# Probabilities times values in plain fp32, two key blocks in the two column halves of the array, inside a two-layer decoder trunk

## The chip, the cores and the metric

The kernel runs on one core of a Trainium2 chip. A time is the device time of one execution in microseconds (us). The kernel before takes 950.52 us, the median of three runs (949.91, 950.52 and 955.53). One more execution was profiled; it took 955.44 us, and every row of the trace below comes from that one. Its span, from the first to the last instruction, is 953.7 us.

## The reference, cut to what matters

The input is 256 tokens of width 1024 in float32. Two layers follow one another, each as half SwiGLU, mixer, half SwiGLU with RMSNorm around every part. The mixer of layer 0 is a pooling mixer. The mixer of layer 1 is an attention with three branches, and the change is in it:

```
proj = h @ w_in                       # q, and k and v of three branches, and gates
o_cmp = softmax(q . k_cmp) @ v_cmp    # 15 compressed keys
o_sel = softmax(q_rot . k_s) @ v_s    # selected blocks
o_win = softmax(q_rot . k_w) @ v_w    # window of 256
o = g0 * o_cmp + g1 * o_sel + g2 * o_win
return o @ w_o
```

There are 16 heads of 64 channels in 4 key groups of 4 heads. With 256 tokens there are 4 blocks of 64, and all are picked, so the selected branch and the window branch are both causal attention over the whole sequence, with their own keys and values. The product of the last softmax with the values, `P @ V`, is what changes in form.

## The kernel before, in words

All weights are float32 in device memory. A product of two float32 matrices is made of three matmuls in the chip's reduced float32 type (fp32r): an operand is split into a high part (a copy on ScalarE that rounds, line 309, or 294 for weights) and a low part (a subtraction on VectorE, line 310 or 295), and `mm3` (lines 304 to 306) adds high by high, high by low and low by high. Some small products are left in plain fp32 instead (lines 740, 758, 769, 802), and so are all transposes, which go through TensorE with an identity matrix (`csm`).

The trunk runs one stage after the other: two SwiGLU parts with the pooling mixer between them, then the SwiGLU part `ffn(1, 0)`, the attention `nsa`, and `ffn(1, 1)`. The attention runs from about 600 to 760 us of the span. Its steps stand in a list written by hand, `NSA_STEPS`; each entry emits one piece of work, and a planner that simulates the engines then orders the instructions of each engine, mostly in the order in which they were emitted, with pieces that are ready earlier let past. The engines work through their own queues in that order.

The names that matter: `t` is one of two halves of 128 queries, `g` one of four key groups (4 heads). `qk(t, g)` computes scores (line 849, each head pair in one half of the array's rows), adds the causal mask (851), takes the maximum on VectorE (853), exponentiates on ScalarE (855) and multiplies by the gate and the reciprocal sum on GpSimd (864). `pv(t, g)` makes `P @ V` for four heads at once into one PSUM tile `o` of 128 x 512. It begins with the compressed branch: GpSimd spreads the compressed probabilities `Pch` and `Pcl` over the heads with a mask (line 882, two instructions of 128 x 512), and two matmuls multiply them by `VC` (line 874). Then it goes through the key blocks of 128 keys, two branches times `t+1` blocks, so 2 blocks for t=0 and 4 for t=1, in all 24 over the eight (t, g). For each block there are four transposes into a PSUM tile (893), a split into `PTh` (309) and `PTl` (310), and two fp32r matmuls of 128 x 512 (874): one for the high, one for the low part of the probabilities. The 128 columns of the stationary operand hold the 64 channels of the high part of V and the 64 of its low part, so the two halves of `o` are added at the end: a copy of the upper half (909), two additions (911) and a split into `OT` (309, 310), which the output projection `out_proj` (304 to 306, `acc<-whi`) reads. Each `yield` ends one step of `NSA_STEPS`.

`v_post` splits V (lines 719), `cmp_v` splits VC (771), `q_pct` splits the compressed probabilities (821). PSUM has two pools of four tiles each; `o` and the transposes come from `psG`, the scores and the accumulators of the output projection from `psA`.

Of the kernel before, what the change touches and what calls it, by code (L numbers as in the profile page):

```python
# [9 lines left out]
F32 = mybir.dt.float32  # L10
F32R = mybir.dt.float32r
BF16 = mybir.dt.bfloat16
AF = mybir.ActivationFunctionType
OP = mybir.AluOpType
# [3 lines left out]
P = 128  # L18
S = 256
NT = S // P  # L20
# [5 lines left out]
NH, HD, NG, NR = 16, 64, 4, 4  # L26
# [72 lines left out]
    ("pv", 0, 1),  # L99
    ("pv", 0, 1),  # L100
    ("vcmp", 1, 0),
    ("pv", 1, 0),
    ("pct", 1, 0),
    ("qk", 1, 0),
    ("qk", 1, 0),
# [1 line left out]
    ("pv", 1, 0),  # L107
    ("pv", 1, 0),
    ("pv", 1, 0),
    ("qk", 1, 1),  # L110
    ("qk", 1, 1),
    ("pv", 1, 0),
    ("rope", 1, 1),
    ("pv", 1, 1),
    ("qk", 1, 1),
    ("qk", 1, 1),
    ("pv", 1, 1),
    ("pc", 1, 1),
    ("qk", 0, 2),
# [2 lines left out]
    ("pv", 1, 1),  # L122
    ("qk", 0, 2),
    ("pv", 1, 1),
    ("pv", 0, 2),
    ("pv", 1, 1),
    ("qk", 0, 3),
    ("qk", 0, 2),
    ("qk", 0, 3),
    ("pv", 0, 2),  # L130
    ("qk", 0, 3),
# [16 lines left out]
    ("out", 0, 0),  # L148
    ("qk", 1, 3),
    ("out", 1, 0),  # L150
    ("pv", 1, 3),
    ("qk", 1, 3),
    ("out", 0, 1),
    ("wo", 2, 0),
    ("out", 0, 2),
# [81 lines left out]
def _trunk(ctx: ExitStack, tc: tile.TileContext, d, out):  # L237
    nc = tc.nc
# [18 lines left out]
    bmask = csm[:, 322:330]  # L257
# [50 lines left out]
    def split(dst, src):  # L308
        return (nc.scalar.activation(dst[0], src, AF.Copy),  # L309
                nc.vector.tensor_tensor(dst[1], src, dst[0].bitcast(F32), op=OP.subtract))  # L310
# [333 lines left out]
    def nsa(pre, g_post, nxt, W0, preload):  # L644
        with tc.tile_pool(name="np", bufs=1, reuse_waits="tile") as np_:
# [11 lines left out]
            W2, W0 = W0  # L657
            gates = [np_.tile([P, 48], F32, name=f"gates{t}") for t in range(NT)]
            kT = tuple(np_.tile([P, NG, 2, S], F32R, name=f"kT{q}") for q in "hl")
            V = np_.tile([P, NT, 2, NG, 2, HD], F32R, name="V")  # L660
            pos = np_.tile([P, 2, 2, 8], F32, name="pos")
            nc.sync.dma_start(pos[:, 0], d["posk"].rearrange("p (a b) -> p a b", a=2))
            nc.sync.dma_start(pos[:, 1], d["posv"].rearrange("p (a b) -> p a b", a=2))
# [50 lines left out]
                            pos[ps, kv, ab, None, None, :].to_broadcast([64, NG, 8 - skip, 8]), op=OP.add)  # L714

            def v_post(o, t):
                ov = o.rearrange("p (b g e) -> p b g e", b=2, g=NG)
                for br in range(2):
                    split([V[:, t, br, :, q, :] for q in range(2)], ov[:, br])

            hidT = np_.tile([P, 2, 2, NG, 16], F32, name="hidT")
            kbd = np_.tile([P, NG, 2, 16], F32, name="kbd")
            VC = [np_.tile([P, 2, HD], F32R, name=f"VC{c}") for c in range(2)]

            def cmp_w(kv):
                src = d[("wk1", "wv1")[kv]]
# [36 lines left out]
            def cmp_v(c):  # L763
                pv = psG.tile([P, HD], F32, name="g")
                rep = np_.tile([P, 2, 2, NR, 16], F32, name="rep", bufs=1)
                for k in range(2):
                    nc.vector.tensor_copy(rep[:, k], hidT[:, 1, k, 2 * c:2 * c + 2, None, :].to_broadcast([P, 2, NR, 16]))
                for k in range(2):
                    nc.tensor.matmul(pv, rep[:, k].rearrange("p a b c -> p (a b c)"), wv2[:, k, :],
                                     start=k == 0, stop=k == 1)  # L770
                split([VC[c][:, q] for q in range(2)], pv)

            qT = {}
            PcT = {}
# [42 lines left out]
            def q_pct(c, t, e):  # L817
                pt = psG.tile([P, P], F32, name="g")
                nc.tensor.transpose(pt, e.rearrange("p a b -> p (a b)"), ident)
                pc = tuple(np_.tile([P, P], F32R, name=f"Pc{q}", bufs=3) for q in "hl")  # L820
                split(pc, pt)
                PcT[c, t] = pc

            OT = [None, None]
# [42 lines left out]
            def pv(t, g):  # L867
                c = g // 2
                Ps = PP[t, g]
                o = psG.tile([P, 2, 2, P], F32, name="g")  # L870

                def mm(A, hl, start, stop):
                    for j in range(2):
                        nc.tensor.matmul(o, A.rearrange("p a b -> p (a b)"), hl[j], start=start and j == 0, stop=stop and j == 1)  # L874

                def PT():
                    return tuple(np_.tile([P, 2, 2, P], F32R, name=f"PT{q}", bufs=2) for q in "hl")

                hl = PT()
                msk = bmask[:, 4 * (g % 2):4 * (g % 2) + 4].rearrange("p (b a) -> p a b", a=2)  # L880
                for q, w in zip(hl, PcT[c, t]):
                    nc.gpsimd.tensor_tensor(q, w[:, None, None, :].bitcast(F32).to_broadcast([P, 2, 2, P]),
                                            msk[:, :, :, None].to_broadcast([P, 2, 2, P]), op=OP.mult)
                mm(VC[c], hl, True, False)
                yield
                nblk = 2 * (t + 1)
                n = 0
                for br in range(2):
                    for kt in range(t + 1):
                        pt = psG.tile([P, 2, 2, P], F32, name="g")  # L890
                        for pr in range(2):
                            for par in range(2):
                                nc.tensor.transpose(pt[:, par, pr, :], Ps[pr][:, par * 2 + br, kt * P:(kt + 1) * P], ident)  # L893
                        hl = PT()
                        split(hl, pt)
                        n += 1
                        mm(V[:, kt, br, g], hl, False, n == nblk)
                        if n < nblk:
                            yield
                if OT[t] is None:  # L900
                    if t == 0:
                        ot = pp.tile([P, 2, 2, KD, P], F32R, name="xT")[:, 0]
                    else:
                        ot = np_.tile([P, 2, KD, P], F32R, name="ot1")
                    OT[t] = [ot[:, i] for i in range(2)]
                ol = np_.tile([P, 512], F32, name="y", bufs=3)
                of = np_.tile([P, 2, P], F32, name="of", bufs=1)
                ol = ol[:HD].rearrange("p (a b q) -> p a b q", a=2, b=2)
                nc.scalar.activation(ol, o[HD:], AF.Copy)
                for par in range(2):  # L910
                    nc.vector.tensor_tensor(of[par * HD:(par + 1) * HD], o[:HD, par], ol[:, par], op=OP.add)
                split([v[:, 2 * g:2 * g + 2, :] for v in OT[t]], of)
                yield
# [33 lines left out]
            def step(kind, i, j):  # L947
# [12 lines left out]
                elif kind == "gates":  # L960
                    gate_fix()
                elif kind == "vpost":
                    v_post(O[4, j], j)
                elif kind == "wcmp":
                    wc[i] = cmp_w(i)
                elif kind == "cmp":
                    hm[i] = cmp_mm(i, wc[i])
                elif kind == "hid":
                    cmp_hid(i, hm[i])
                elif kind == "kcmp":  # L970
                    cmp_k()
                elif kind == "vcmp":
                    cmp_v(i)
                elif kind == "q":
                    qs[i, j] = q_evac(O[3 + 2 * i, j])
                elif kind == "nope":
                    qn[i, j] = q_nope(qs[i, j])
                elif kind == "rope":
                    q_rope(i, j, qs[i, j])
                elif kind == "pc":  # L980
                    ec[i, j] = q_cmp(i, j, qn[i, j])
                elif kind == "pct":
                    q_pct(i, j, ec[i, j])
                elif kind == "wo":
                    wo.append(ksplit(piece(d["wo"][:, i * 2048:(i + 1) * 2048], step=512), 2))
                    if i == 3:
                        nxt.load()
                elif kind == "out":
                    out_proj(i, j)
# [18 lines left out]
    for c, hs, ls in ((0, [], pre[0].s), (1, [], pre[0].s), (2, pre[0].h[0], pre[0].h[0]), (3, pre[0].h[0], pre[0].h[0])):  # L1008
        v = [q[:, c * 512:(c + 1) * 512] for q in W[0]]
# [11 lines left out]
    W = ffn(0, 1, pre[2], 5, pre[3], W, pre_ffn(1, 0))  # L1021
    W = ffn(1, 0, pre[3], 7, pre[4], W, pre_nsa())
    W = nsa(pre[4], 9, pre[5], W, pre_ffn(1, 1))
    ffn(1, 1, pre[5], 11, None, W, None)

# [14 lines left out]
```

## Time and profile before

| what | value |
|---|---|
| runs | 949.91, 950.52, 955.53 us, median 950.52 us |
| profiled execution | 955.44 us, its span 953.7 us |
| TensorE matmul busy | 937.3 us, 98% of the span |
| VectorE busy | 666.1 us, 70% |
| ScalarE busy | 475.7 us, 50% |
| GpSimd busy | 82.2 us, 9% |
| mean granted TensorE clock | 0.988 |

In the profile PE stands for TensorE's matmuls, PEld for its weight loads, DVE for VectorE, ACT for ScalarE, POOL for GpSimd and SP for SyncE. Matmuls are pipelined, so the length of a record is longer than the distance to the next one; the distance between starts is what a matmul costs in a row of them. A granted clock (PEclk) of 1.00 is 2.4 GHz, one of 0.50 is 1.2 GHz. "128*64" in a matmul is the rows and columns of the array that it uses, and "128x512" the moving operand.

### The profile page before, as it was taken

To read this page: it belongs to the slowest core of one execution; us is meant where nothing else is said; L and a number is where in the kernel's file an instruction comes from. 1 tells how busy PE (TensorE), PEld (TensorE's weight loads), DVE (VectorE), ACT (ScalarE), POOL (GpSimd) and SP (SyncE) were. 2 spreads that over 40 slices of the span, in tenths; PEclk is the share of its full clock that TensorE was granted. 3 is DMA by queue.
4 is the path that set the end of the run, shared out by engine and by line. 5 is a ranking of instruction groups with operands and counts; after the bars stand their busy time and mean duration, and the time that the engine had idled before them with its cause. 6 is when DMAs were issued, how large, how long until landed. Compare 5 with 4: busy or idle time off the path is not lost.

```text
span 953.7 us, 13074 instructions
## 1 busy us (share of the span) xinstructions
PE 937.3 (98%) x4882; PEld 783.3 (82%) x4882; DVE 666.1 (70%) x977; ACT 475.7 (50%) x812; POOL 82.2 (9%) x78
## 2 busy tenths in 40 slices
PE   8999999999999999999999999999999999999997
PEld 5888888877888888888888888888677678888885
DVE  6866677786867666758666667688965868666653
ACT  7654444355645344545544444545765666544421
POOL 1000001131000000110000002002445110000000
PEclk9999999999999999999999999999889899999999
DMA  8865675325866565258665553572200358665511
GB/s 318 283 223 195 216 239 178 124 98 176 271 216 221 185 207 184 90 173 279 211 214 182 186 194 98 204 265 90 88 1 1 112 193 284 213 211 186 193 45 44
DMA packets 47457, 168.96 MB, mean 177 GB/s; under 512 B 5529, under 2 KB 6041, under 8 KB 46882
## 3 DMA queue, kind: packets, MB, share of 16 engines
q1 hardware_dynamic: 47394, 168.13, 52.7%
q8 instruction: 38, 0.62, 0.3%
q14 instruction: 25, 0.20, 0.1%
HBM read 167.06 MB, written 1.05 MB: 176 GB/s over the span
## 4 chain that ended last, share of the span: by engine, by line
PE 52%; DVE 4%; issue 1%; ACT 1%; DMA 0%; POOL 0%; DVEq 0%; POOLq 0%; ACTq 0%
PE g L501 14%; PE g L502 7%; PE acc L304 5%; PE acc L306 5%; PE acc L305 5%; PE g L304 3%; PE g L306 2%; PE g L305 2%; PE acc L849 2%; PE g L874 2%; PE g L469 1%; PE g L893 1%; DVE wlo L295 1%; PE acc L851 1%; DVE x L350 1%
## 5 line engine op out<-in xcount | busy, mean ns | idle before, releaser
L501 PE MATMUL g<-xT,whi 128*128 128x512 f32 x1152 | 406.0, 394 | 0.0
L502 PE MATMUL g<-xT,wlo 128*128 128x256 f32 x1152 | 325.1, 282 | 0.0
L294 ACT ACTIVATE whi<-raw 128x1024 fp32r<-128x1024 f32 (+2 forms) x252 | 204.9, 863 | 157.7 <-issue 41.8
L295 DVE TENSOR_TENSOR wlo<-raw,whi 128x1024 fp32r<-128x1024 f32 (+2 forms) x252 | 244.5, 1012 | 46.6 <-ACT whi L294 46.3
L501 PEld LDWEIGHTS g<-xT,whi 128*128 128x128 f32 x1152 | 216.3, 188 | 49.5
L502 PEld LDWEIGHTS g<-xT,wlo 128*128 128x128 f32 x1152 | 216.5, 188 | 1.4
L295 DVE TENSOR_TENSOR dlo<-raw,dhi 128x1024 fp32r<-128x1024 f32 (+1 forms) x128 | 119.3, 955 | 100.0 <-ACT dhi L294 99.9
L294 ACT ACTIVATE dhi<-raw 128x1024 fp32r<-128x1024 f32 (+1 forms) x128 | 103.9, 842 | 153.9 <-DMA raw<-in_wd 145.2
L438 DVE TENSOR_REDUCE sg<-g 128x256 f32<-128x512 f32 x144 | 98.1, 687 | 58.1 <-PE g L502 58.0
L304 PE MATMUL acc<-dhi,hTh 128*128 128x512 f32 x288 | 112.3, 390 | 0.0
L305 PE MATMUL acc<-dlo,hTh 128*128 128x512 f32 x288 | 112.0, 389 | 0.0
L306 PE MATMUL acc<-dhi,hTl 128*128 128x512 f32 x288 | 111.4, 389 | 0.0
L304 PE MATMUL g<-whi,xT 128*128 128x512 f32 (+2 forms) x168 | 64.4, 385 | 1.3 <-ACT xT L309 0.7
L341 POOL TENSOR_TENSOR rs<-ms,neghalf 128x1 f32<-128x1 f32 x24 | 13.2, 548 | 602.2 <-DVE ms L339 602.2
L305 PE MATMUL g<-wlo,xT 128*128 128x512 f32 (+2 forms) x168 | 63.9, 381 | 0.0
L306 PE MATMUL g<-whi,xT 128*128 128x512 f32 (+2 forms) x168 | 63.6, 380 | 0.0
L306 PEld LDWEIGHTS acc<-dhi,hTl 128*128 128x128 f32 x288 | 54.1, 188 | 11.4
L304 PEld LDWEIGHTS acc<-dhi,hTh 128*128 128x128 f32 x288 | 54.1, 188 | 11.2
L305 PEld LDWEIGHTS acc<-dlo,hTh 128*128 128x128 f32 x288 | 54.0, 188 | 9.9
L304 PEld LDWEIGHTS g<-whi,xT 128*128 128x128 f32 x168 | 31.9, 190 | 8.4 <-ACT xT L309 2.0
L305 PEld LDWEIGHTS g<-wlo,xT 128*128 128x128 f32 x168 | 32.0, 191 | 6.5 <-DVE wlo L295 0.8
L306 PEld LDWEIGHTS g<-whi,xT 128*128 128x128 f32 x168 | 32.0, 190 | 6.5 <-DVE xT L310 0.7
(191 smaller groups left out, 1044.0 us busy)
## 6 DMA issues: line engine op xcount, KB each, us to landing
raw<-in_wu SPq DMA_DIRECT2D x88, 512.0 KB, 4.6
raw<-in_wd SPq DMA_DIRECT2D x88, 512.0 KB, 4.5
raw<-in_wg SPq DMA_DIRECT2D x86, 512.0 KB, 3.9
raw<-in_win SPq DMA_DIRECT2D x18, 512.0 KB, 4.5
gain<-in_gains SPq DMA_DIRECT2D x11, 512.0 KB, 3.7
raw<-in_wo SPq DMA_DIRECT2D x8, 512.0 KB, 5.0
raw<-in_win SPq DMA_DIRECT2D x4, 304.0 KB, 2.9
raw<-in_wg SPq DMA_DIRECT2D x4, 256.0 KB, 3.7
```

The costliest lines, as they stand in the source:

```text
L294: nc.scalar.activation(hi[:, n + a:n + b], r[:, a:b], AF.Copy)
L295: nc.vector.tensor_tensor(lo[:, n + a:n + b], r[:, a:b], hi[:, n + a:n + b].bitcast(F32), op=OP.subtract)
L304: nc.tensor.matmul(o, A[0], B[0], start=start, stop=False)
L305: nc.tensor.matmul(o, A[0], B[1], start=False, stop=False)
L306: return nc.tensor.matmul(o, A[1], B[0], start=False, stop=stop)
L341: nc.gpsimd.tensor_tensor(r, v, neghalf, op=OP.pow)
L350: nc.vector.scalar_tensor_tensor(x[t][:, H[h]], fg[:, H[h]], r, x[t][:, H[h]], op0=OP.mult, op1=OP.add)
L438: nc.vector.tensor_reduce(dst, o.rearrange("p a b -> p b a"), axis=AX.X, op=OP.add)
L501: nc.tensor.matmul(o, hi, pre.xx[:, :, k, :], start=k == 0, stop=False)
L502: nc.tensor.matmul(o[:, 1, :], lo, xT[0][:, k, :], start=False, stop=k == KD - 1)
L849: nc.tensor.matmul(o, A[i], B[j], start=i + j == 0, stop=False)
L874: nc.tensor.matmul(o, A.rearrange("p a b -> p (a b)"), hl[j], start=start and j == 0, stop=stop and j == 1)
```

## The change

The low and high parts of probabilities and values go away. `V`, `VC`, the compressed probabilities and the transposed probabilities `PT` are plain fp32 copies. `pv` takes the key blocks in pairs: eight transposes into two PSUM tiles, one copied out by ScalarE and the other by VectorE, a `yield`, then two fp32 matmuls of 128 x 512 with 64 stationary columns each, one into partitions 0 to 63 of `o` and the other into partitions 64 to 127, which are the two column halves of the array, and a `yield`. The compressed branch moves from the first step of `pv` to its last: one GpSimd instruction in place of two, and two fp32 matmuls of 128 x 256, one in each column half. The end of `pv`, which adds the two halves of `o`, stays. The number of steps of a `pv` stays too (3 for t=0, 5 for t=1), but in `NSA_STEPS` some `pv` steps move back by one to four entries, past `qk`, `rope` and `pct` steps; no step that issues a DMA is moved.

```diff
 NSA_STEPS = [
...
-    ("pv", 1, 0),
     ("pct", 1, 0),
     ("qk", 1, 0),
     ("qk", 1, 0),
...
     ("pv", 1, 0),
     ("pv", 1, 0),
+    ("pv", 1, 0),
     ("qk", 1, 1),
...
-            V = np_.tile([P, NT, 2, NG, 2, HD], F32R, name="V")
+            V = np_.tile([P, NT, 2, NG, HD], F32, name="V")
...
             def v_post(o, t):
-                ov = o.rearrange("p (b g e) -> p b g e", b=2, g=NG)
-                for br in range(2):
-                    split([V[:, t, br, :, q, :] for q in range(2)], ov[:, br])
+                nc.scalar.activation(V[:, t].rearrange("p b g e -> p (b g e)"), o, AF.Copy)
...
-                split([VC[c][:, q] for q in range(2)], pv)
+                nc.vector.tensor_copy(VC[c], pv)
...
-                split(pc, pt)
+                nc.scalar.activation(pc, pt, AF.Copy)
...
             def pv(t, g):
                 c = g // 2
                 Ps = PP[t, g]
                 o = psG.tile([P, 2, 2, P], F32, name="g")
...
+                of32 = o.rearrange("p a b q -> p (a b q)")
+                blocks = [(br, kt) for br in range(2) for kt in range(t + 1)]
+                for n in range(0, len(blocks), 2):
+                    PT = []
+                    for i, (br, kt) in enumerate(blocks[n:n + 2]):
                         pt = psG.tile([P, 2, 2, P], F32, name="g")
                         for pr in range(2):
                             for par in range(2):
                                 nc.tensor.transpose(pt[:, par, pr, :], Ps[pr][:, par * 2 + br, kt * P:(kt + 1) * P], ident)
-                        hl = PT()
-                        split(hl, pt)
-                        n += 1
-                        mm(V[:, kt, br, g], hl, False, n == nblk)
-                        if n < nblk:
-                            yield
+                        q = np_.tile([P, 512], F32, name="PT", bufs=6)
+                        v = pt.rearrange("p a b q -> p (a b q)")
+                        if i == 0:
+                            nc.scalar.activation(q, v, AF.Copy)
+                        else:
+                            nc.vector.tensor_copy(q, v)
+                        PT.append(q)
+                    yield
+                    for i, (br, kt) in enumerate(blocks[n:n + 2]):
+                        nc.tensor.matmul(of32[i * HD:(i + 1) * HD], V[:, kt, br, g], PT[i], start=n == 0, stop=False)
+                    yield
+                q = np_.tile([P, 2, 2, P], F32, name="PT", bufs=6)
+                msk = bmask[:, 4 * (g % 2):4 * (g % 2) + 4].rearrange("p (b a) -> p a b", a=2)
+                nc.gpsimd.tensor_tensor(q, PcT[c, t][:, None, None, :].to_broadcast([P, 2, 2, P]),
+                                        msk[:, :, :, None].to_broadcast([P, 2, 2, P]), op=OP.mult)
+                for i in range(2):
+                    nc.tensor.matmul(o[i * HD:(i + 1) * HD, i].rearrange("p b q -> p (b q)"), VC[c],
+                                     q[:, i].rearrange("p b q -> p (b q)"), start=False, stop=True)
```

## Rows read from the trace of the kernel before

**Rows 1.** The page's first two parts: busy time of each engine, and the granted clock in the span in 40 slices of 23.8 us (tenths).

```profile
PE 937.3 (98%) x4882; PEld 783.3 (82%) x4882; DVE 666.1 (70%) x977; ACT 475.7 (50%) x812; POOL 82.2 (9%) x78
...
PEclk9999999999999999999999999999889899999999
```

**Rows 2.** Busy time in stretches of the attention. Columns: the stretch, its length, the busy us of each engine with the count of instructions, the granted TensorE clock, the DMA share and GB/s.

```profile
676.00:683.90 7.90, 7.90 (x36) 5.00 (x35) 7.87 (x17) 6.32 (x22) 5.44 (x4) 1.00 0.01 3
683.90:684.90 1.00, 0.16 (x1) 0.00 (x0) 1.00 (x3) 1.00 (x5) 0.45 (x1) 0.98 0.00 0
684.90:698.50 13.60, 13.47 (x45) 10.55 (x45) 9.43 (x26) 6.92 (x25) 6.38 (x5) 0.50 0.00 1
...
743.00:749.70 6.70, 5.08 (x25) 3.20 (x23) 6.70 (x12) 5.03 (x12) 1.82 (x2) 1.00 0.64 221
749.70:756.50 6.80, 6.19 (x16) 4.67 (x17) 4.06 (x10) 2.30 (x6) 0.55 (x1) 0.50 0.00 0
```

**Rows 3.** The chain of waits from 676 to 690 us, in order of time: start, length, what (pieces with the same name merged).

```profile
682.53 1.77 issue
...
685.03 0.80 PE g L874
```

**Rows 4.** TensorE's matmuls in order of time from 683 to 686 and from 745 to 752.5 us, those with idle time of the engine before them (in brackets, with what ended it).

```profile
685.03 0.80 PE L874 MATMUL g<-PTl,V 128*128 128x512 f32 x1 [0.97 <-DVE PTl L310]
...
747.79 0.50 PE L874 MATMUL g<-PTl,V 128*128 128x512 f32 x1 [0.46 <-DVE PTl L310]
...
749.75 0.80 PE L874 MATMUL g<-PTl,V 128*128 128x512 f32 x1 [1.02 <-DVE PTl L310]
...
752.39 0.80 PE L304 MATMUL acc<-whi,ot 128*128 128x512 f32 x1 [0.56 <-ACT ot L309]
```

**Rows 5.** VectorE from 660 to 686 us in order of time: start, length, line, operation, count.

```profile
682.49 1.88 DVE L813 TENSOR_TENSOR cst<-cst,gates 128x8 f32<-128x8 f32 x1
684.30 0.68 DVE L310 TENSOR_TENSOR PTl<-g,PTh 128x512 fp32r<-128x512 f32 x1
```

**Rows 6.** GpSimd from 676 to 686 us in order of time.

```profile
680.58 1.10 POOL L882 TENSOR_TENSOR PTl<-Pcl,csm 128x512 fp32r<-128x512 f32 x1
682.46 1.89 POOL L864 TENSOR_TENSOR big<-big,ar 128x1024 f32<-128x1024 f32 x1 [0.79 <-DVE cst L812]
```

**Rows 7.** TensorE's matmuls in order of time from 709.6 to 711 us: a run of fp32r matmuls of 128 x 512.

```profile
709.65 0.39 PE L874 MATMUL g<-PTl,V 128*128 128x512 f32 x1
709.88 0.40 PE L874 MATMUL g<-PTh,V 128*128 128x512 f32 x1
710.11 0.40 PE L874 MATMUL g<-PTl,V 128*128 128x512 f32 x1
```

**Rows 8.** The instructions of line 740 (fp32, 64 stationary columns, alternately in the one and the other column half): length in ns (least, median, longest), first and last start.

```profile
L740 PE MATMUL g<-chi,big x64: 272/273/323, 627.5 to 646.8; 128*64 128x128 f32 x64
L740 PE MATMUL g<-clo,big x64: 272/273/273, 629.3 to 648.6; 128*64 128x128 f32 x64
```

**Rows 9.** TensorE's matmuls around the first of them, in windows that end at 627.545, 627.552 and 627.71 us, and where they end; runs with one name are merged, their length goes to the end of the last.

```profile
627.01 0.60 PE L694 MATMUL g<-csm,fx 128*128 128x128 f32 x4
...
627.54 0.32 PE L740 MATMUL g<-chi,big 128*64 128x128 f32 x1
...
627.54 0.33 PE L740 MATMUL g<-chi,big 128*64 128x128 f32 x2
...
627.54 0.43 PE L740 MATMUL g<-chi,big 128*64 128x128 f32 x3
...
630.65 0.61 PE L740 MATMUL g<-clo,big 128*64 128x128 f32 x8
631.19 0.55 PE L705 MATMUL g<-csm,y 128*128 128x128 f32 x3
```

**Rows 10.** The chain of waits from 600 to 780 us: two runs of TensorE, start and the time that they carry the chain.

```profile
645.18 3.64 PE g L740 x64
...
732.44 0.87 PE g L893 x8
```

**Rows 11.** Groups of instructions from 655 to 760 us, shapes apart: busy us, mean ns of one, idle time before and what ended it.

```profile
L310 DVE TENSOR_TENSOR PTl<-g,PTh 128x512 fp32r<-128x512 f32 x24 | 16.3, 684 | 2.1 <-ACT PTh L309 1.7 <-PE g L874 0.2
...
L806 DVE TENSOR_TENSOR ce<-g,csm 128x128 f32<-128x128 f32 x3 | 0.9, 287 | 0.1
...
L753 DVE COPY hidT<-g 128x120 f32<-128x120 f32 x1 | 0.3, 283 | 3.0 <-PE g L752 3.0
...
L309 ACT ACTIVATE PTh<-g 128x512 fp32r<-128x512 f32 x24 | 14.2, 598 | 6.7 <-PE g L893 4.4 <-POOL big L864 1.3 <-ACT whi L294 0.6
```

**Rows 12.** The tile V: the instructions that split it (length in ns, least, median, longest, first and last start), and the last of those that waited for one (us, times).

```profile
L309 ACT ACTIVATE V<-g x4: 366/377/395, 627.0 to 630.5; 128x256 fp32r<-128x256 f32 x4
L310 DVE TENSOR_TENSOR V<-g,V x4: 416/418/418, 628.3 to 632.2; 128x256 fp32r<-128x256 f32 x4
...
  PE g L304: 0.5, 1
```

**Rows 13.** TensorE's matmuls in order of time from 700.3 to 702 us: the two matmuls of a key block with other work between them.

```profile
700.61 0.60 PE L794 MATMUL g<-csm,y 128*128 128x128 f32 x4
700.96 0.48 PE L874 MATMUL g<-PTh,V 128*128 128x512 f32 x1
701.37 0.38 PE L849 MATMUL acc<-kTh,qh 64*128 64x256 f32 x1
```

More of the change, by code (lines that the diff above doesn't have):

```diff
@@ L113 @@
     ("rope", 1, 1),
-    ("pv", 1, 1),
     ("qk", 1, 1),
     ("qk", 1, 1),
+    ("pv", 1, 1),
     ("pv", 1, 1),
@@ L124 @@
     ("pv", 1, 1),
-    ("pv", 0, 2),
     ("pv", 1, 1),
@@ L128 @@
     ("qk", 0, 2),
+    ("pv", 0, 2),
     ("qk", 0, 3),
@@ L150 @@
     ("out", 1, 0),
+    ("qk", 1, 3),
     ("pv", 1, 3),
-    ("qk", 1, 3),
     ("out", 0, 1),
@@ L716, in v_post @@
             def v_post(o, t):
-                ov = o.rearrange("p (b g e) -> p b g e", b=2, g=NG)
-                for br in range(2):
-                    split([V[:, t, br, :, q, :] for q in range(2)], ov[:, br])
+                nc.scalar.activation(V[:, t].rearrange("p b g e -> p (b g e)"), o, AF.Copy)
             hidT = np_.tile([P, 2, 2, NG, 16], F32, name="hidT")
             kbd = np_.tile([P, NG, 2, 16], F32, name="kbd")
-            VC = [np_.tile([P, 2, HD], F32R, name=f"VC{c}") for c in range(2)]
+            VC = [np_.tile([P, HD], F32, name=f"VC{c}") for c in range(2)]
             def cmp_w(kv):
@@ L819, in q_pct @@
                 nc.tensor.transpose(pt, e.rearrange("p a b -> p (a b)"), ident)
-                pc = tuple(np_.tile([P, P], F32R, name=f"Pc{q}", bufs=3) for q in "hl")
-                split(pc, pt)
+                pc = np_.tile([P, P], F32, name="Pc", bufs=3)
+                nc.scalar.activation(pc, pt, AF.Copy)
                 PcT[c, t] = pc
@@ L870, in pv @@
                 o = psG.tile([P, 2, 2, P], F32, name="g")
[L872 to L877, printed above, removed]
-                hl = PT()
[L880 to L884, printed above, removed]
-                yield
[L886 to L889, printed above, removed]
+                of32 = o.rearrange("p a b q -> p (a b q)")
[3 more added lines that the diff above has]
+                    for i, (br, kt) in enumerate(blocks[n:n + 2]):
                         pt = psG.tile([P, 2, 2, P], F32, name="g")
@@ L893, in pv @@
                                 nc.tensor.transpose(pt[:, par, pr, :], Ps[pr][:, par * 2 + br, kt * P:(kt + 1) * P], ident)
-                        hl = PT()
-                        split(hl, pt)
-                        n += 1
-                        mm(V[:, kt, br, g], hl, False, n == nblk)
-                        if n < nblk:
-                            yield
+                        q = np_.tile([P, 512], F32, name="PT", bufs=6)
[16 more added lines that the diff above has]
+                                     q[:, i].rearrange("p b q -> p (b q)"), start=False, stop=True)
                 if OT[t] is None:
```

## The prediction

> **What bounds the kernel now.** I read the page first. TensorE's matmuls are busy for 98% of the span, the vector engine for 70%, and the granted clock is full in all slices but three or four [rows 1]. So a gain must come from TensorE's own work, from its few waits, or from the clock; work taken from another engine is worth nothing where that engine only runs beside TensorE.
>
> Then I cut the attention into stretches [rows 2]. From 676 to 683.9 us the vector engine is busy for 7.87 of 7.90 us: it is the bound there. TensorE still runs, but then stands for 0.97 us [rows 4]. Behind that the clock falls to 0.50 (1.2 GHz) for 13.6 us, and it falls once more for 6.8 us behind the stretch from 743 to 749.7, where TensorE was busy for only 5.08 of 6.70 us and the vector engine for all of it.
>
> The chain of waits names the cause of the first stand [rows 3]: TensorE's next matmul waits for the low part of the probabilities, PTl, which is late because the vector engine took 1.88 us for a multiplication of 8 elements per partition [rows 5], which ended when GpSimd's multiplication of 1.89 us ended [rows 6]. In the second place TensorE waits 0.46 and 1.02 us for PTl and 0.56 us for the split of the output [rows 4]. The change removes PTl altogether.
>
> **TensorE's work.** Removed: two fp32r matmuls for each of 24 key blocks and two for each of 8 compressed branches, 64 in all. In a row they start 0.23 us apart [rows 7]: 64 x 0.23 = 14.7 us.
>
> Added: 12 pairs of fp32 matmuls of 512 columns and 8 pairs of 256. Line 740 does the same with 128 columns, 64 matmuls alternating between the two column halves. They leave 128 records [rows 8], so a fp32 matmul runs in two passes. A stream of 64 records lasts 3.64 us [rows 10], so two records per 0.114 us; the two halves work at the same time, since a single fp32 transpose of 128 columns takes 0.87 / 8 = 0.109 us with the whole array [rows 10]. A pair has two such passes: 2 x 0.114 = 0.228 us at 128 columns, 0.91 at 512, 0.46 at 256. That is 12 x 0.91 + 8 x 0.46 = 14.6 us. In columns nothing is won or lost.
>
> What comes on top is the change of the array's form. The four transposes before line 740 start at 627.01, so the last near 627.34, and the next could start at 627.45; the first half-width record starts at 627.54: 0.09 lost. The second pair starts at 627.54 + 0.43 - 0.27 = 627.70, 0.16 behind the first where 0.11 is usual: 0.05. At the end the last record starts near 630.65 + 0.61 - 0.27 = 630.99, the next transposes at 631.19, 0.09 late, and their own start loses 0.05 more [rows 9]. So 0.28 us per group of half-width matmuls that stands alone. The change makes 20 pairs; the last pair of values and the compressed pair of one (t, g) can stand together, so 12 to 20 groups. I take 13, as nearly all last steps of a `pv` follow their matmul step directly in the list: 13 x 0.28 = 3.6 us, less the 0.1 of the columns, **+3.5 us**. The ends are +2.6 (12 groups, and the columns at 0.109, which saves 0.7) and +5.5 (20 groups).
>
> Here a measured ratio of the Trainium skill speaks against the change: its page "TensorE: Matmul & The Clock Gate", section "Measured speedup vs the span model", gives 2.38 for three column groups, not 3. As an estimate from that figure, two halves would be worth 1.59 in place of 2, and the sum would have 3.8 us more. Line 740 shows 0.114 against 0.109 us [rows 10], so nearly the full 2, and I keep that.
>
> **The other engines.** The vector engine loses 24 subtractions of 684 ns and gains 12 copies of 512 columns out of PSUM [rows 11]. No such copy is in the trace; the small copy from PSUM costs what a subtraction of its size does (283 against 287 ns) [rows 11], so I take 0.68; the ends are 0 and 0.75. That is 8 us less. ScalarE loses 12 of 24 copies of 598 ns, 7 us less. GpSimd loses 8 of its 16 masks of about 1.1 us [rows 6]; the vector engine, which is held up beside GpSimd's long ones [rows 5, 6], gains a little more. All of this runs beside TensorE and is worth nothing by itself; its worth is in the waits.
>
> V's split on two engines becomes one ScalarE copy per half. TensorE waits 0.5 us for the last subtraction [rows 12]; two copies of some 0.6 us [rows 11] stand for 1.5 us of halves on ScalarE and 1.7 on the vector engine. I take -0.5, ends 0 and -0.7: weight splits on ScalarE could come late in its place. The split of VC and the compressed probabilities is small and hidden under scores and projections; without that cover it costs the 0.3 us of a small copy [rows 11].
>
> The stand at 684: one copy where two PTl were, and one mask less ahead of it. I take -1.0 of the 1.0 that TensorE is idle, ends 0 and -1.0. What is late next is the softmax of the compressed branch, whose instructions on the vector engine stay. At the end of the attention the waits of 0.46, 1.02 and 0.56 us [rows 4] sum to 2.0; a `pv` of t=1 has two rounds of transpose, copy, matmul now, not four. But the normalization of the first half of the tokens still shares the vector engine there, and a pair needs both copies. I take half, -1.1 with the small waits beside them, ends 0 and -2.2.
>
> **The moved steps** issue no DMA. Later `pv` steps let `qk` steps go first on TensorE and ScalarE; the compressed mask moves behind the pairs on GpSimd's queue, past multiplications of line 864, and is covered by the pair's 0.9 us and GpSimd's low load (9%) [rows 1]. Uncovered it would cost its 1.1 us. A new wait: the second matmul of a pair needs the vector engine's copy, in its queue behind maxima and weight subtractions; queued behind that matmul on TensorE are the scores and transposes of the next steps, and the exponentials on ScalarE wait for those. A pair also holds two of four PSUM tiles beside `o`; with two `pv` open the next transposes wait for a copy, up to 0.6 us in each of the 4 later rounds of t=1, that is 0 to 2.4 us. I take 0, since a tile is now read by one engine and not by two in turn.
>
> **The clock.** 13.6 us at half clock with TensorE busy for 13.47 of them cost 6.8 us, and the second stretch 3.1 [rows 2]. Both begin directly behind the waits for PTl. I take the first as gone, -6.8, and the second as staying, since half of its waits stay. The ends are -9.9 and +6.8 (one more such stretch).
>
> **The sum** against the profiled execution, 955.4 us: + 3.5 - 0.5 - 1.0 - 1.1 - 6.8 = **949.5 us**. That execution lies 4.9 us above the median of 950.5. What differs isn't in one trace; it is less than the clock's 6.8 us, so the median run may have less of that stretch. From the median, without the clock, the sum is 950.5 + 0.9 = 951.4; with all of it 944.6. I keep 949.5, between the two.
>
> **Rivals.**
> (a) The clock falls all the same: the sparse stretch of small matmuls ahead of 684 stays as it is. 951.4 from the median, 956.3 from the profiled execution. For it: the change takes TensorE's wait away, not its small matmuls; against: the clock fell nowhere else in the attention, and small matmuls are all over it [rows 1, 2].
> (b) Slower: the pairs are torn apart. The two matmuls wait for copies on two engines, and the planner may put other work between them, as it does with the two matmuls of a block now [rows 13]. A matmul alone in its half takes 2 x 4 x 0.109 = 0.87 us, so a torn pair costs 2 x 0.87 - 0.91 = 0.83 more and one more group, 0.28: 1.1 us. From 951.4 it decides from 8 torn pairs of the 12 on (960.2); with all 20, the short ones at 0.7, it is 970. Against it: the transposes of a pair end only 0.44 us apart (4 x 0.109), and one matmul lasts longer than that.
> (c) The passes start only in the order in which they are issued. Then the second matmul's first pass waits for the first's second, and a pair takes three passes of 0.44, not two: 12 x 0.40 + 8 x 0.20 = 6.4 us more, 956 to 958. The window that ends 7 ns after one that holds one record of line 740 holds two [rows 9], so both halves began together. [...]
> (d) Faster: all waits and both stretches go, PE at its low end: 955.4 + 2.6 - 0.7 - 1.0 - 2.2 - 9.9 = 944.2, or 939.3 from the median.
>
> **Chances.** Forecast 0.43; (a) 0.25; (b) 0.12; (c) 0.05; (d) 0.10; waits for PSUM tiles and other mishaps 0.05, 952 to 960. One per cent of 950.5 is 9.5 us, about what can be told from no change. Below 941.0: (d) and the low edge of the forecast, 0.12. Above 960.0: (b), 0.12. Within: 0.76. The range 939 to 961 takes in the forecast, (a), (c) and (d), and of (b) only its near edge.
>
> **What would show it.** Right: 12 pairs of fp32 records starting within some ns, 0.91 us per pair; full clock from 685 to 698; no wait of TensorE near 684; some 8 us less on the vector engine. Wrong: the two halves at different times with other lines between; a third half-clock stretch; waits of transposes for copies. The prediction is wrong if TensorE's added work is beyond 5.5 us or the clock falls in new places.

## The result and the profile after

The changed kernel takes **961.63 us** (median of four runs, 959.07 to 966.78); the kernel before, beside it, 952.14. The ratio is 1.0098, with a 95% interval of 1.0068 to 1.0127: 9.5 us slower, where the prediction had no change, most likely 1 us faster. The profiled execution took 963.41 us, its span is 961.6 us. These are its page's busy times and granted clock, beside [rows 1]:

```profile
PE 945.1 (98%) x4898; PEld 775.1 (81%) x4898; DVE 647.7 (67%) x957; ACT 469.5 (49%) x796; POOL 74.5 (8%) x70
...
PEclk9999999989999999999999999999999999999999
```

VectorE lost 18.4 us, ScalarE 6.2, GpSimd 7.7. TensorE gained 7.8 although the clock is better than before. The stretches of [rows 2] in the changed kernel, with the same columns:

```profile
676.00:683.90 7.90, 7.90 (x40) 4.81 (x40) 6.70 (x22) 6.74 (x25) 5.26 (x4) 1.00 0.18 71
683.90:684.90 1.00, 1.00 (x4) 0.48 (x4) 1.00 (x4) 0.64 (x4) 0.58 (x1) 1.00 0.00 0
684.90:698.50 13.60, 13.60 (x65) 7.56 (x63) 6.85 (x21) 8.03 (x32) 6.02 (x4) 1.00 0.00 1
743.00:749.70 6.70, 6.70 (x28) 3.99 (x27) 3.10 (x5) 2.64 (x5) 1.05 (x1) 1.00 0.44 153
749.70:756.50 6.80, 6.80 (x31) 3.73 (x31) 3.70 (x7) 4.21 (x9) 0.00 (x0) 1.00 0.31 96
```

TensorE stands nowhere from 676 to 698.5 us, VectorE is full in none of the long stretches, and the clock stays at 1.00 (2.4 GHz) where it had fallen to 0.50 (1.2 GHz). In this execution it fell in two other places instead, from 205.3 to 212.1 us in an earlier part and from 768.5 to 771.9 us behind the attention. So what the change was expected to relieve in these stretches is relieved, and the loss is work on TensorE itself. Its matmuls in order of time, two windows of the changed kernel; line 888 holds the matmuls of V, 895 those of VC, and each fp32 matmul leaves two records:

```profile
677.35 0.38 PE L849 MATMUL acc<-amaskr,identr 128*128 128x256 f32 x1
677.66 1.08 PE L888 MATMUL g<-PT,V 128*64 128x512 f32 x4
678.57 0.60 PE L895 MATMUL g<-PT,VC 128*64 128x256 f32 x4
...
685.47 0.38 PE L849 MATMUL acc<-amaskr,identr 128*128 128x256 f32 x1
685.79 1.07 PE L888 MATMUL g<-PT,V 128*64 128x512 f32 x2
686.79 0.66 PE L767 MATMUL g<-wv,rep 128*128 128x64 f32 x4
687.38 1.07 PE L888 MATMUL g<-PT,V 128*64 128x512 f32 x2
688.38 0.38 PE L847 MATMUL acc<-kTh,qh 64*128 64x256 f32 x1
```

The first pair stands together: four records, and the next work starts 0.91 us later, as forecast. The second is **torn**: one matmul alone (1.00 us to the next start), then line 767, then the other alone (1.00 us). Of the 12 pairs, 10 are torn; only the first and the last are not. No torn pair was torn by a late copy that TensorE waited for. The copies that the torn pair above needed, from VectorE's and ScalarE's order of time:

```profile
683.00 0.68 DVE L884 COPY PT<-g 128x512 f32<-128x512 f32 x1
```

```profile
682.06 0.60 ACT L882 ACTIVATE PT<-g 128x512 f32<-128x512 f32 x1 [0.39 <-PE g L878]
```

Both were done by 683.68, 2.1 us before the first of the two matmuls ran. In 9 of the 10 torn pairs both copies had ended before the first matmul started. The order on TensorE was fixed when the kernel was built. My reading is that in the planner's model ScalarE's copy, that of the first block, is ready earlier, so it lets the first matmul go and fills in other work; the model itself is in no trace, and the runs with the order and the engines exchanged, below, are what bears on it.

TensorE's waits in the changed kernel from 600 to 785 us, by what ended them (us, times, longest):

```profile
PE g L469 <- ACT xT L309: 2.5, 1, 2.5
PE acc L304 <- ACT ot L309: 1.0, 1, 1.0
```

Before, they summed to 4.2 us (2.4 and 0.4 for PTl and PTh, 0.6 for `ot`, 0.5 for V, 0.3 for xT). All those for PTl, PTh and V are gone; 2.5 us for the input of `ffn(1, 1)` are new.

### The profile page after: what moved, and what is told of

It reads as the page before. It is cut to its first block, busy times and chain, and to the rows that moved or that the text cites. A ratio compares the mean times of both kernels' runs of the same rounds, so it can differ in the third digit from the quotient of the medians.

```text
span 961.6 us, 13055 instructions
## 1 busy us (share of the span) xinstructions
PE 945.1 (98%) x4898; PEld 775.1 (81%) x4898; DVE 647.7 (67%) x957; ACT 469.5 (49%) x796; POOL 74.5 (8%) x70
## 4 chain that ended last, share of the span: by engine, by line
PE 55%; DVE 1%; ACT 1%; issue 0%; POOL 0%; DVEq 0%; POOLq 0%; ACTq 0%
PE g L501 14%; PE g L502 7%; PE acc L304 5%; PE acc L305 5%; PE acc L306 5%; PE g L304 3%; PE g L306 3%; PE g L305 3%; PE g L888 2%; PE acc L847 2%; PE g L878 1%; PE g L469 1%; PE acc L849 1%; PE g L738 1%; ACT whi L294 0%; DVE x L350 0%
```

## The experiments

The theory after this reading: torn pairs are the loss, about 9.5 us over 10 pairs, so 0.95 each. Rivals: the halves themselves, the moved steps, or something else in the new copies. To compare kernels whose clock falls differently from run to run, I also give a **full-clock length**: a run's span times its mean granted clock, median over the runs. The clock is given to three decimals, which is worth about 0.5 us. More counts that the length comes out shorter where the clock was lower: of ten runs of one kernel further down, those at a clock of 0.997 and above give 945.3 to 946.2 us, and those at 0.988 943.6 and 944.1. So it does not tell kernels apart by less than some 2 us where their clocks differ. The kernel before has 942.3 to 943.2 us in the batches below, the changed kernel 955.6: 13 us apart, of which the clock gives back some 4.

**Pairs joined by the copies.** Each copy fills half of the columns of both blocks, so that both matmuls of a pair become ready with the later copy:

```diff
-                    PT = []
-                    for i, (br, kt) in enumerate(blocks[n:n + 2]):
+                    PT = np_.tile([P, 2, 2, 2, P], F32, name="PT", bufs=3)
+                    for par in range(2):
                         pt = psG.tile([P, 2, 2, P], F32, name="g")
-                        for pr in range(2):
-                            for par in range(2):
-                                nc.tensor.transpose(pt[:, par, pr, :], ...
+                        for i, (br, kt) in enumerate(blocks[n:n + 2]):
+                            for pr in range(2):
+                                nc.tensor.transpose(pt[:, i, pr, :], ...
...
-                        nc.tensor.matmul(of32[i * HD:(i + 1) * HD], V[:, kt, br, g], PT[i], ...
+                        nc.tensor.matmul(o[i * HD:(i + 1) * HD], V[:, kt, br, g], PT[:, :, i], ...
```

> The changed kernel, with each pair's two fp32 matmuls both made to need both copies: each copy takes one half of the columns of both key blocks, so the planner sees both matmuls ready at once and keeps them next to each other. Theory A (torn pairs): in the trace of the changed kernel 10 of 12 pairs have other work between their two matmuls, and each such matmul stands alone for 0.48 + 0.52 us with about 0.2 us of lost starts around it. Joined, a pair takes about 1.0 + 0.2, so 10 x 1.2 = 12 us go: 961.6 - 12 = 950, between 946 and 953. Theory B (the change of the array's form and the longer passes are the cost, joined or not): only the lost starts of 10 groups go, 2 to 3 us, 958 to 960. Theory C (the wait of 2.8 us ahead of the next stage and the order of the steps are the cost): within 2 us of 961.6.

Measured: 952.16 us, before 951.93, ratio 1.0008 [0.9983, 1.0032]; full-clock length 946.6. All 12 pairs stand together, and the last pair of each (t, g) has the VC pair right behind it:

```profile
683.85 1.08 PE L885 MATMUL g<-PT,V 128*64 128x512 f32 x4
684.76 0.60 PE L892 MATMUL g<-PQ,VC 128*64 128x256 f32 x4
...
690.99 1.08 PE L885 MATMUL g<-PT,V 128*64 128x512 f32 x4 [1.47 <-DVE PT L882]
```

Of the 9.5 us some 9 are gone. The last line shows a price of joining: a wait of 1.47 us for VectorE's copy. It is not the only new wait: TensorE's waits from 600 to 785 us sum to 7.3 us here, 4.0 of them ahead of line 364 for the normalisation at the end of the attention and 1.4 for weight splits, where the changed kernel has 3.5 in all.

**The moved steps alone**: the kernel before with the change's list and nothing else of it.

```diff
 NSA_STEPS = [
...
-    ("pv", 1, 0),
     ("pct", 1, 0),
...
+    ("pv", 1, 0),
     ("qk", 1, 1),
```

> The kernel before with nothing but the changed list of steps. Theory A: the order is not the cost, within 3 us of the kernel before (952). Theory C: the moved steps cost 4 us or more, 956 and above.

Measured: 953.89, ratio 1.0016 [0.9998, 1.0033]; full-clock length 943.9, before 943.2. The list is worth nothing that can be told.

**No column halves, copies as in the change.** V is stored with 64 columns of zeros beside its 64 (the result is the same), so that each matmul uses the whole width:

```diff
-                        nc.tensor.matmul(of32[i * HD:(i + 1) * HD], V[:, kt, br, g], PT[i], start=n == 0, stop=False)
+                        nc.tensor.matmul(of32, V[:, kt, br, g].rearrange("p a e -> p (a e)"), PT[i], start=n == 0 and i == 0, stop=False)
```

> The changed kernel, but the stationary operand of a key block has 128 columns, the upper 64 of them zero, so no matmul of a key block is in a column half; the copies stay as in the change, and a matmul alone takes as many columns as before. The compressed pairs stay in the halves. Theory A: a torn matmul gains nothing from its half, so nothing is lost in columns; 24 x 0.87 us in place of about 22 x 1.0 + 1.0, and the lost starts of about 0.25 us at some 20 of them go: 4 to 7 us less than the changed kernel, 955 to 958. If the halves did work together somewhere in the torn ones, or the change of form cost nothing, it would be at 961 or above.

Measured: 953.48, ratio 1.0012 [0.9994, 1.003], full-clock length 948.4. It is below the expected 955 to 958: a kernel that gives up the halves for V is 8 us faster than one that has them and tears them. By starts of records a whole-width matmul takes 0.86 us (674.595, 675.025 and 675.454 for the first three passes), a torn half 1.00. Yet all 48 records of V take 20.91 us here and 21.56 in the change, only 0.65 less, as the two joined pairs of the change give most of the difference back. From a mask to a V matmul it is 0.196 us on the average of 8, in the change 0.314, and all masks together take 1.3 us less. The scores take 2.2 us less: seven times their matmuls for two head pairs start side by side, about 4 ns apart, and in the change only four or five times. So the planner's new order paired other matmuls too, and this kernel alone does not price the halves. Of the 6.9 us between the two kernels, from the first matmul of the scores to the first of line 501 in `ffn(1, 1)` with time at half clock counted half, 2.7 are not parted.

**Joined and whole width**, the copies of the first experiment and the V of the one just told; against the joined halves:

```diff
-                        nc.tensor.matmul(o[i * HD:(i + 1) * HD], V[:, kt, br, g], PT[:, :, i], ...
+                        nc.tensor.matmul(o, V[:, kt, br, g].rearrange("p a e -> p (a e)"), PT[:, :, i], ...
```

> Both edits together: the two matmuls of a pair next to each other, each over the whole width with zeros in the upper half, so one after the other and with no change of form. Against the first run of this group it shows what the column halves give to a joined pair. Theory A: 24 x 0.87 = 20.9 us where the joined pairs in halves take 12 x 1.2 = 14.4: 5 to 7 us slower than the joined kernel, 955 to 957. Theory B: equal to or faster than the joined kernel.

Measured: 958.31, ratio 1.0074 [1.0056, 1.0092], a miss; full-clock length 951.8, 5.2 above the joined halves. So joined halves are worth 5 us against the same copies in whole width, each in the order that the planner made of it. Twelve pairs at 2 x 0.86 - 0.91 = 0.81 us would be 9.7, and by the starts of their records the matmuls of V do take 21.42 us here for 11.31 there. Against that stand waits of TensorE, 5.2 us for 7.3, and the scores with their masks, 2.5 us less in this order.

**A part of the pairs torn.** The joined form for t=0 alone, and for t=1 alone; by blocks otherwise. The tile of the joined copies has one buffer in the first and two in the second (three in the joined kernel). The second of the two:

```diff
+                        if t == 0:
                             nc.tensor.matmul(of32[i * HD:(i + 1) * HD], V[:, kt, br, g], PT[i], ...
+                        else:
+                            nc.tensor.matmul(o[i * HD:(i + 1) * HD], V[:, kt, br, g], PT[:, :, i], ...
```

> Copies by column halves (pairs joined) for the first 128 queries only, and by blocks, as in the change, for the other 128; the planner's order then has 5 torn pairs of 12. Theory A: the cost goes with the count of torn pairs. From 10 torn (961.6) to none (952.2) it is 0.94 us for each, so 952.2 + 5 x 0.94 = 956.9, between 955 and 959. Theory B (something else in the joined version, such as the form of the copies, made the gain): 952 or 961, not between.

> The other way round: joined for the second 128 queries, by blocks for the first; 2 torn pairs in the planner's order. Theory A: 952.2 + 2 x 0.94 = 954.1, between 952 and 956, and not above the run with five.

Measured: 5 torn, 959.38, ratio 1.0072 [1.0045, 1.0099], full-clock length 950.9; 2 torn, 950.15, ratio **0.9969 [0.9956, 0.9983]**, full-clock length 944.5. Both miss their expectations, on opposite sides, so the number of torn pairs is not all. The first of the two stands 6.0 us for the normalisation at the end of the attention, but the second stands 4.5 us for it as well:

```profile
PE g L364 <- DVE fx L394: 6.0, 1, 6.0
PE g L901 <- ACT PT L883: 1.0, 1, 1.0
PE g L304 <- ACT xT L309: 0.2, 1, 0.2
```

All waits of TensorE in that part are 7.2 us with five torn pairs and 4.7 with two, and the records of V take 15.32 and 12.37 us. Together that is 5.5 of the 6.4 us between their full-clock lengths.

**Priority for the end of a `pv`, and for the copies**, both on the joined kernel: the copy of the upper half, the additions and the split in one (the edit raises the priority in the last `pv` alone), the two PT copies in the other get a higher priority in the planner.

```diff
+                with tc.high_priority(1000 if (t, g) == (1, 3) else 1):
                     nc.scalar.activation(ol, o[HD:], AF.Copy)
...
+                        with tc.high_priority(200):
                             if par == 0:
                                 nc.scalar.activation(PT[:, par], pt, AF.Copy)
```

> The joined kernel with a higher priority for the copy, the additions and the split at the end of each pv. In the joined kernel TensorE waits 2.7 us ahead of the transposes of the next stage while the last output of pv lies behind weight splits in ScalarE's queue, so that the last output projections can't fill the gap. If that queue is the cause, 1 to 2.5 us go: 949.5 to 951.5. If the chain of the normalization alone sets the gap, no change within 1 us (952).

> The joined kernel with a higher priority for the two copies of each pair. A joined pair waits for both; in the joined kernel TensorE waits 1.5 us near 691 for a copy behind maxima on the vector engine. If copies are what the joined pairs are late for, 1 to 2 us go, 950 to 951; against that, later maxima delay the exponentials and with them the next transposes: then it is the same or up to 3 us slower.

Measured: 951.15, ratio 0.9993 [0.9972, 1.0013], and 951.81, ratio 0.9994 [0.9976, 1.0012]. Neither differs from the joined kernel, and neither could: in the three traces TensorE, VectorE, ScalarE and GpSimd run the same operations on tiles of the same names in the same order, so the priority moved nothing. The two are further sets of runs of the joined kernel (full-clock lengths 945.9 and 946.3). TensorE's wait near 690 us is 0.93 and 1.47 us in them; ahead of the copy VectorE works through additions and maxima without a pause. Whether an earlier place in the queue would help is not tested by them.

**Only the order of the two matmuls.** The sharpest one: the changed kernel, its transposes, copies and list untouched, but of a pair the second block's matmul, whose copy is taken to be ready later, is issued first.

```diff
-                    for i, (br, kt) in enumerate(blocks[n:n + 2]):
+                    for i, (br, kt) in reversed(list(enumerate(blocks[n:n + 2]))):
                         nc.tensor.matmul(of32[i * HD:(i + 1) * HD], V[:, kt, br, g], PT[i], start=n == 0, stop=False)
```

> The changed kernel with one edit: of the two matmuls of a pair, the one of the second block, whose copy VectorE makes and which is ready later, is issued first. Copies, transposes, columns and list stay as in the change; in the order of TensorE's instructions 11 of the 12 pairs then stand together (2 do in the change). Theory (torn pairs are the loss, 0.95 us each by the measured 961.6 - 952.2 over 10 pairs): 9 pairs fewer torn, 8.6 us less, 951 to 954. Rival (the joined variant gained by its other arrangement of the copies, each copy holding half the columns of both blocks, and not by the joining): no such gain, 959 to 962. Rival (joined pairs wait for the later copy and give it back): 955 to 958.

Measured: 949.91, before 953.62, ratio 0.9975 [0.9948, 1.0002]; full-clock length 945.3, 10.3 us under the change; the time is below the expected 951 to 954. Here are its page's busy times, a pair in order of time, and its waits:

```profile
PE 935.2 (98%) x4898; PEld 775.1 (81%) x4898; DVE 647.1 (68%) x957; ACT 468.5 (49%) x796; POOL 75.8 (8%) x70
```

```profile
687.26 1.08 PE L888 MATMUL g<-PT,V 128*64 128x512 f32 x4
688.17 0.60 PE L895 MATMUL g<-PT,VC 128*64 128x256 f32 x4
```

```profile
PE g L469 <- ACT xT L309: 2.5, 1, 2.5
PE g L888 <- DVE PT L884: 1.3, 2, 1.0
PE g L304 <- ACT xT L309: 0.2, 1, 0.2
```

Eleven of 12 pairs stand together. VectorE, ScalarE and GpSimd do what they do in the change, to within 1.3 us; TensorE is busy for 9.9 us less. By the distances between starts, with time at half clock counted half, the 48 records of V take 12.25 us here and 21.56 in the change: 9.3 us for 9 pairs, 1.03 each. This settles it: the loss is the tearing, and the rival of the other copies falls. The counts of torn pairs that the expectations here name ahead of the runs (5, 2, 1 and 7) are those of the traces, so the order on TensorE is the one that was built.

**The engines of the two copies swapped**, VectorE for the first block, ScalarE for the second; 7 pairs are torn.

```diff
-                        if i == 0:
+                        if i == 1:
                             nc.scalar.activation(q, v, AF.Copy)
```

> The changed kernel with the engines of the two copies swapped: VectorE makes the first block's copy, ScalarE the second's, so that the two are ready closer together. In the order of TensorE's instructions 7 pairs of 12 are torn. Theory (0.95 us for each torn pair): 961.6 - 3 x 0.95 = 958.8, between 957 and 960.5. Rival (the engine of the copies is what counts, VectorE's copy being the late one): as much as with all pairs joined, 951 to 954. Rival (the number of torn pairs does not count): 961 to 963.

Measured: 960.57, ratio 1.007 [1.004, 1.0099], just above its interval; full-clock length 951.8, which is 3.8 under the change for 3 pairs. In time only 1.1 us are left of it, as the clock was lower (0.993 in the median, 0.9955 in the change's).

The by-block and joined kernels with half-width V have these full-clock lengths, by the count of their torn pairs:

| torn of 12 | 0 | 1 | 2 | 5 | 7 | 10 |
|---|---|---|---|---|---|---|
| full-clock length, us | 946.6 | 945.3 | 944.5 | 950.9 | 951.8 | 955.6 |

From two torn pairs on the length rises with the count. The first three differ by 2.1 us, at the edge of what this length can tell, and the longest of them has the longest waits, 7.3 us against 4.0 and 4.7.

**The reversed order once more, in more runs**, and beside it with the priority for the end of a `pv` that is shown above.

> The kernel with the second block's matmul issued first once more, in more rounds, for a narrower interval: 949 to 952, ratio to before between 0.994 and 1.000 if the joining is worth the 10 us that the first look showed; a ratio of 1.000 or more would mean that the relief of the waits and of the clock is all paid back.

> The same kernel, with the end of a pv (copy of the upper half, additions, split) given priority on ScalarE and VectorE. If the waits of TensorE at the end of the attention (1.3 us for the last copies, 2.5 us for the next part's input) come from late instructions of that end, 1 to 2 us less than the kernel beside it, 948 to 950.5. If they come from the length of the normalisation itself, no difference, as in the joined variant (951.2 against 952.2).

Measured: 952.57, before 953.79, ratio 0.9995 [0.997, 1.002], full-clock length 945.1, the time just above its expectation; with the priority 951.91, ratio 0.9984 [0.9963, 1.0006], full-clock length 945.3. The 949.91 of the first set was a lucky draw of the clock: the two sets of runs of the same kernel have the same full-clock length, and the medians of their clocks are 0.997 and 0.994. The wait for `ffn(1, 1)` stayed with the priority, but here too every engine's order is the same with and without it, so this is a third set of runs of one kernel and does not tell whether the wait is a matter of a place in a queue. With the pairs together the change is **no different** from the kernel before within what can be told. Only the variant with two torn pairs lies below it with its whole interval, by 0.3%. Its full-clock length is above that of the kernel before, 944.5 for 942.6, so what it gains is the clock's; and as it is the best of several, I would not build on that without a second set of runs.

## Why the prediction was wrong, and where it was right

The step that failed is the argument **against rival (b)**: "the transposes of a pair end only 0.44 us apart (4 x 0.109), and one matmul lasts longer than that". From there the forecast went on with 12 pairs together and 12 to 20 groups. That argument holds for an engine that takes what comes; TensorE takes its instructions in an order fixed when the kernel is built, and the planner had other work ready for the gap. [Rows 13] showed it doing just this to the two matmuls of a block, which shared even their transposes; I gave it 0.12. The trace shows that the gap is not one of readiness: 9 of the 10 torn pairs had both copies beforehand.

- **The price of a torn pair**, 0.83 + 0.28 = 1.1 us, was right: 1.03 on the V matmuls themselves by the reversed order (1.14 by full-clock length, 10.3 / 9). A lone matmul takes 1.00 us, not the 0.87 of the columns; the 0.13 is the change of form that the sum had put in a term of its own. Rival (b) put 8 torn pairs at 960.2, and so 10 at 962.4; the 10 pairs gave 961.6.
- **A joined pair** costs 0.91 us to the next start (677.66 to 678.57, and 687.26 to 688.17), as worked out from line 740.
- **The Trainium skill's 2.38 for three column groups** (page "TensorE: Matmul & The Clock Gate", section "Measured speedup vs the span model"): the estimate of 1.59 for two halves, worked out from it, is not what the trace shows. A joined pair takes 0.91 us where two whole-width matmuls take 2 x 0.86, which is 1.9.
- **The Trainium skill's "strict FIFO, no reordering"** (the same page, section "The mechanism") is said of matmuls, and of the passes of a fp32 matmul it says nothing. The two matmuls of a pair do start in order, 7 ns apart (677.659 and 677.666 us); the second passes of both start at 678.139 and 678.146 us, so the second matmul did not wait for the first one's second pass. On whole matmuls the trace agrees with it; carried over to the passes it would be rival (c), and there the trace does not.
- **PE's term with pairs together**, +3.5 (2.6 to 5.5): from the first matmul of the scores to the first of line 501 in `ffn(1, 1)`, with time at half clock counted half, TensorE takes 119.14 us before and 123.09 with the order reversed, 3.95 more. Its waits in that part are 3.7 us before (2.4 + 0.4 + 0.6 + 0.3) and 4.0 with the order reversed (2.5 + 1.3 + 0.2). That leaves 3.65 us of work: the forecast's size. The changed kernel takes 133.03 us, 10 us beyond that.
- **The stand at 684 and V's wait**: gone, -1.0 and -0.5, as forecast.
- **The end of the attention**, forecast -1.1, was mis-sized. With the stand at 684 it should have brought 2.1 us; the waits of the whole attention came out at 3.5 us in the change and 4.0 with the order reversed, for 3.7 before. The waits for PTl went, but 2.5 us for `ffn(1, 1)` came in their place, and with the order reversed 1.3 us of the joined pairs for VectorE's copy. In the trace before, the transposes of line 364 (757.86 us) are followed by the rest of the output projection, and ScalarE splits xT (760.28 us) beside it:

```profile
757.86 1.04 PE L364 MATMUL g<-csm,fx 128*128 128x128 f32 x8
758.65 0.47 PE L304 MATMUL acc<-whi,ot 128*128 128x512 f32 x1
758.96 0.39 PE L305 MATMUL acc<-wlo,ot 128*128 128x512 f32 x1
```

In the change, and likewise with the order reversed, that projection is already done when line 364 comes, and nothing covers the split:

```profile
764.38 0.39 PE L306 MATMUL acc<-whi,ot 128*128 128x512 f32 x1
764.61 1.03 PE L364 MATMUL g<-csm,fx 128*128 128x128 f32 x8
768.19 1.84 PE L469 MATMUL g<-whi,xT 128*128 128x512 f32 x4 [2.54 <-ACT xT L309]
```

- **The clock**, -6.8: the stretch of [rows 2] behind 684.9 us is gone from this profile, but the clock fell in two new places, one of the signs of being wrong, and the size is a matter of chance from run to run. By span times one minus mean clock the kernel before loses 7.9 to 9.6 us on the average of a batch, the change 4.8, the reversed order 4.2 and 6.4. So the relief is some 2 to 5 us, about half of the forecast; rival (a) was half right.
- **VectorE's share**, forecast as 8 us less, came out at 18.4 less. The copies of PT for its subtractions are 8.2 of it, as worked out. The low parts of V, VC and the compressed probabilities are some 3 more, and other instructions came out shorter: the multiplications of `cst` by the gates, the one of 1.88 us [rows 5] among them, take 0.66 us in all for 3.50.
- **The sum without tearing**, 949.5 from one profiled execution and 951.4 from the median without the clock, is where the kernels with joined pairs came out (952.16, 949.91, 952.57). In part that is luck: without the clock the sum was 0.9 us above the kernel before, and their full-clock lengths are 2.4 to 3.4 above it; the clock's relief gave that back.

## What to carry to other kernels

Two matmuls that are fast only side by side must be adjacent in the engine's instruction order, and here that was decided when the kernel was built: look at that order, not at whether their inputs come close together on the chip. If the inputs come from two engines, issue the one first whose input the planner expects later, or let both depend on the same copies. A work term that counts on such a pairing needs the rival "not paired" at a chance drawn from how the planner treated the nearest pair in the trace.

## What the runs showed of the hardware that was not expected

- A lone fp32 matmul of 512 columns in one column half takes 0.480 us for its first pass (685.786 to 686.266) and 0.523 for its second, to the next start; one in whole width 0.43 for each. So alone in a half it is slower than in the whole array. The excess is at its ends: in a joined pair the first passes take 0.480 us as well, and the second, with half-width work behind them, 0.429 (678.139 to 678.568).
- GpSimd's multiplication of 128 x 512 (line 356) takes from 1.27 to 4.08 us among the ten in the kernel before. The last of the ten took 2.88 us there and in the change, 4.68 with the order reversed and 6.49 in the kernel joined by the copies, from 761.57 us on. What stood beside it was not varied, so the cause is open:

```profile
761.57 6.49 POOL L356 TENSOR_TENSOR fx<-x,gain 128x512 f32<-128x512 f32 x1 [1.38 <-DVE x L350]
```

- The clock's falls come and go between runs of one kernel: the ten runs of the reversed order lie between mean clocks of 0.988 and 0.999, and their times between 948.1 and 957.4 us, while span times clock stays within 943.6 and 946.2 us, the lower values at the lower clocks. For changes of one per cent the full-clock length tells kernels apart that the times leave unclear; for a quarter of that it does not.
